# Gate products and sums moved to GpSimd, one product's bank emptied early, and the latent norm interleaved with the context's keys

## The chip, the cores and the metric

The kernel runs on one core of a Trainium2 chip. The metric is the device time of one execution in microseconds. A core has a matrix engine (PE, with its weight loads listed as PEld), a vector engine (DVE), a scalar engine (ACT), GpSimd (POOL) and DMA engines that are fed from queues; SP only issues DMAs, ACT and POOL issue DMAs beside their own work. Each engine takes its instructions in one fixed order and stands where an instruction has to wait.

## The reference

A trunk of two layers over 256 latent tokens and 256 context tokens of width 1024. Layer 0 is a bidirectional mLSTM with a gated ConvFFN, for context and latents; layer 1 is multi-head latent attention with a gated ConvFFN, for the latents alone. What the change touches is this:

```
x1 = layer_norm(ALPHA * x + gate * mixer(h))             # for both streams, layer 0
f  = (silu(dwconv(h2 @ W_gate)) * (h2 @ W_up)) @ W_out
x2 = layer_norm(ALPHA * x1 + gate * f)
# layer 1, latents: q, k, v from h3 = x2 * (1 + scale) + shift, context keys and values from hc
ckv, k_rope = split(h @ w_dkv);  k, v = split(rms_norm(ckv) @ w_ukv)
q = rms_norm(h3 @ w_dq) @ w_uq
```

Each layer norm ends in `* g + b`. The kernel folds that into the modulation for the next product and, apart from it, writes the full `x = z * g + b` to memory for the next residual.

## The kernel before, in words

Float32 products are made of three passes with split operands: every weight tile (128 x 1024) arrives by DMA as `raw`, ACT copies it to a rounded high part (L323) and DVE subtracts to get the low part (L326); `mm3` (L383 to L385) then multiplies high by high, high by low and low by high. So each weight tile costs an ACT pass, a DVE pass, and 12 matmuls of 512 columns on PE. A class `Stream` holds the order of the tiles, the ring of `raw` buffers and three split buffers `w` (NB = 3). A `raw` buffer comes free when DVE has split it; then SP issues the next load.

The tile framework has a scheduler: it orders each engine's instructions by its own estimate of costs, except where `keep_in_program_order` (here `pin`) holds an instruction in the place where the program wrote it. Background work (norms, transposes) is written as generators, and `tick` runs one step of them between products.

**`w_fout0`** (from L1365) is the output product of layer 0's ConvFFN, done as a Strassen-like scheme of seven products on 512-column halves. First come four products side by side, `yt2`, `y11`, `yt3` and `yt1`, six tiles each, into four pairs of PSUM banks p6, p1, p7 and p5 (all eight banks). Then the pairs are combined: ACT copies p1 to `u1` (L1434), DVE forms `u2`, `u3`, `v` and the final `u4` from PSUM (L1437 to L1446). Then follow `y21` (six tiles, 66 matmuls), `y22` (66) and `yt4` (three tiles, then three more kept for the end), each into a new pair of banks. A generator `residual` does, for each of eight half blocks, `u = u * gate` (L1454) and `z = ALPHA * z + u` (L1455) on DVE, one block per tick; for the blocks of `vv` it also takes the norm's statistics (`bn_stats`, L1457). `add` (L1464 to L1466) brings in `y21`, `y22` and at the very end `yt4`. `z_norm` (L1502 on) normalises, `ln_T` (L1191 on) transposes on PE and splits.

The weight tiles of `yt4` need a sum in memory: SP loads a stored partial sum (`t2d`, L278) and when that has landed POOL issues a DMA that adds the weights to it (L279). These issues stand in POOL's order.

**Layer 1's start.** `mla_ctx` makes the context's compressed keys, `ukn(0)` the context's keys of eight heads (48 matmuls of 256 columns), `uv` its values. Before, `ukn(0)` and `uv((0,))` are written first, and then four ticks of the latents' norm (`mid(1)`, that is `norm1`: add `yt4`, normalise, transpose, split into `hl`). Then `mla` multiplies `hl` by `w_dkv` (48 matmuls of 320 columns, `dkv`) and by `w_dq` (48 of 384, `dq`), transposes the latents' compressed keys (`dkv_T`, L1572 to L1577) and makes the latents' keys with `ukn(1)`.

**`ln_x`** (L1217) writes `z * g + b`: four products (L1227) and four sums (L1228) on DVE per call, each followed by a DMA from POOL. It is called with `ln` = 0 for both streams of layer 0's first norm, with 1 for the latents' second norm and with 2 in layer 1. **`ffn_in`** (L1292) in layer 1 uses for pair 0 of the columns three matmuls of 256 columns, and from pair 1 on two matmuls (L1320: one of 512 columns that serves high and low at once, one of 256), whose two halves ACT copies (L1323) and DVE adds (L1324).

Of the kernel before, what the change touches and what calls it, by code (L numbers as in the profile page):

```python
# [11 lines left out]
ALU = mybir.AluOpType  # L12
# [342 lines left out]
class K:  # L355
# [861 lines left out]
    def ln_x(self, ln, zs, dst):  # L1217


        nc = self.nc  # L1220
        g = self.bcast(self.a["ln_g"][ln:ln + 1, :], "gr")
        b = self.bcast(self.a["ln_b"][ln:ln + 1, :], "br")
        yield
        for t in range(2):
            for h in range(2):
                c = slice(h * 512, (h + 1) * 512)
                nc.vector.tensor_tensor(zs[t][:, c], zs[t][:, c], g[h], op=ALU.mult)  # L1227
                nc.vector.tensor_tensor(zs[t][:, c], zs[t][:, c], b[h], op=ALU.add)  # L1228
                nc.gpsimd.dma_start(dst[t][:, c], zs[t][:, c])
                yield  # L1230

# [60 lines left out]
    def ffn_in(self, l, hT, n, nt, pre=(), both=None):  # L1292

        nc, st = self.nc, self.st
        cw, cb = self.smc("fcw%d" % l), self.smc("fcb%d" % l)
        key = "fin%d" % l
        acts = []
        pre = list(pre)
        for p in range(NF):
            pss = []  # L1300
            for j in range(2):
                if pre:
                    w, ps = pre.pop(0)
                    self.ffn_half(ps, w, hT, 1)
                    if not pre:
                        st.unhold()
                else:
                    w = st.use((key, p, j))
                    ps = self.ps("fin")
                    two = ps.rearrange("p (a t) -> p a t", a=2)  # L1310
                    for k in range(8):
                        c = slice(k * 128, (k + 1) * 128)
                        hi, lo = hT(k)
                        if both is None or p == 0:
                            self.mm3(ps[:, :n], (w[0][:, c], w[1][:, c]), (hi, lo), k == 0, k == 7)
                            continue

                        mms = [(two, w[0][:, c], both(k)), (ps[:, :n], w[1][:, c], hi)]
                        for i, (o, a, b) in enumerate(mms if k < 7 else mms[::-1]):
                            nc.tensor.matmul(o, a, b, start=k == 0 and i == 0, stop=k == 7 and i == 1)  # L1320
                    if both is not None and p > 0:
                        t = self.s2("fs")
                        nc.scalar.copy(t[:, n:2 * n], ps[:, n:2 * n])  # L1323
                        nc.vector.tensor_tensor(t[:, :n], ps[:, :n], t[:, n:2 * n], op=ALU.add)  # L1324
                        ps = t
                pss.append(ps)
                self.tick(nt, ADA_F if p else 0)
            tmp = self.s2("fg")
            self.conv(pss[0], [cw[:, j * NF + p:j * NF + p + 1] for j in range(3)], cb[:, p:p + 1], tmp, n)
            nc.vector.tensor_tensor(tmp[:, :n], tmp[:, :n], pss[1][:, :n], op=ALU.mult)  # L1330
            if l == 0:
                if p % 2:
                    self.act_sums(p // 2, acts.pop(), tmp)
                else:
                    acts.append(tmp)
                continue
            a = self.u("act")
            nc.scalar.copy(a[:, 0, :n], tmp[:, :n])
            nc.vector.tensor_sub(a[:, 1, :n], tmp[:, :n], a[:, 0, :n])
            acts.append(a)  # L1340
        return acts
# [23 lines left out]
    def w_fout0(self, x1d, mid):  # L1365
# [25 lines left out]
        def prod(ps, x, w, i, bs=(0, 1)):  # L1391
            for h in range(2 if i < 5 else 1):
                j = 2 * i + h
                a = A[x, j]
                for b in bs:
                    ts = slice(b * 128, (b + 1) * 128)
                    cs = slice(h * 512, (h + 1) * 512)
                    self.mm3(ps[b], (a[:, 0, ts], a[:, 1, ts]), (w[0][:, cs], w[1][:, cs]), j == 0, j == 10)
# [4 lines left out]
        lo, hi = slice(0, 512), slice(512, 1024)  # L1403
        p6, p1, p7, p5 = [pair() for _ in range(4)]
        n = 0
        for i in range(6):
            for name, ps, x in (("yt2", p6, "S2"), ("y11", p1, "1"), ("yt3", p7, "S3"), ("yt1", p5, "S1")):
                w = st.use((name, 0, i))
                prod(ps, x, w, i)
                for f in ("S2", "1", "S3", "S1"):  # L1410
                    if f == x:
                        for j in (2 * i, 2 * i + 1):
                            A.pop((f, j), None)
                self.tick(1)
                if n >= 8:
                    operand()
                if n == 14:
                    gate = []
                    for g in (1, 0):
                        t = self.uf("gate")  # L1420
                        nc.gpsimd.dma_start(t, self.gd[0, 5][g:g + 1, :].to_broadcast([128, 1024]))
                        gate.append(t)
                if n >= 16 and n % 2 == 0:
                    if n == 16:
                        z = []
                    t = self.uf("z")
                    nc.gpsimd.dma_start(t, x1d[len(z)])
                    z.append(t)
                n += 1
        stats = [self.tiny(12, "st").rearrange("p (a b) -> p a b", b=6) for _ in range(4)]  # L1430
        u1, u3, u4, vv = [], [], [], []
        for b in range(2):
            u = self.s2("u1")
            nc.scalar.copy(u, p1[b])  # L1434
            u1.append(u)
            u = self.s2("u2")
            nc.vector.tensor_tensor(u, p6[b], u1[b], op=ALU.add)  # L1437
            u4.append(u)
# [7 lines left out]
            nc.vector.tensor_tensor(u4[b], p5[b], u4[b], op=ALU.subtract)  # L1446
            vv.append(v)

        def residual():

            for us, g, c in ((u1, 0, lo), (u4, 0, hi), (u3, 1, lo), (vv, 1, hi)):
                for b in range(2):
                    zz = z[2 * g + b]
                    nc.vector.tensor_tensor(us[b], us[b], gate[g][:, c], op=ALU.mult)  # L1454
                    nc.vector.scalar_tensor_tensor(zz[:, c], zz[:, c], ALPHA, us[b], op0=ALU.mult, op1=ALU.add)  # L1455
                    if us is vv:
                        nc.vector.bn_stats(stats[2 * g + b][:, 1], zz[:, c])  # L1457
                    yield

        def add(g, c, ps):  # L1460
            for b in range(2):
# [7 lines left out]
        for i in range(6):  # L1469
            w = st.use(("y21", 0, i))  # L1470
            prod(ps, "2", w, i)
            if i == 1:
                self.bg.append(residual())
            self.tick(1)
            operand()
        add(0, lo, ps)
        ps = pair()
        for i in range(6):
            w = st.use(("y22", 0, i))
            prod(ps, "S4", w, i)  # L1480
            self.tick(1)
            operand()
        self.drain()
# [4 lines left out]
        for i in range(6 - YTAIL):  # L1488
            w = st.use(("yt4", 0, i))
            prod(ps, "3", w, i)  # L1490
            self.tick(2)
        self.drain()
        mid(None, None, None)
        ws = [(i, st.use(("yt4", 0, i), hold=True)) for i in range(6 - YTAIL, 6)]
# [85 lines left out]
                nc.scalar.copy(self.krT[:, 0, cs], p)  # L1580
                nc.vector.tensor_sub(self.krT[0:64, 1, cs], p[0:64], self.krT[0:64, 0, cs])

    def ukn(self, g):

        cs = slice(g * 256, (g + 1) * 256)
        for h in range(H1):
            w = self.wk[h // 4]
            if h % 2 == 0:
                ps = self.ps("kn")
            hs = slice((h % 2) * 256, (h % 2 + 1) * 256)  # L1590
            for k in range(2):
                c = slice((h % 4) * 256 + k * 128, (h % 4) * 256 + (k + 1) * 128)
                self.mm3(ps[:, hs], (w[0][:, c], w[1][:, c]), (self.ckT[k][:, 0, cs], self.ckT[k][:, 1, cs]),
                         k == 0, k == 1)
            u = self.kn[h]
            self.split(u[:, 0, cs], u[:, 1, cs], ps[:, hs])

    def uv(self, ts):
        for t in ts:
# [33 lines left out]
    def mla(self, hl):  # L1633
# [7 lines left out]
        for c in range(4):  # L1641
            w = st.use(("dq", 0, c))
            self.tick()
            for kk in range(2):
                k = 2 * c + kk
                hi, lo = hl(k)
                cs = slice(kk * 384, (kk + 1) * 384)
                for t in range(2):
                    ts = slice(t * 128, (t + 1) * 128)
                    self.mm3(pss[t][:, :384], (hi[:, ts], lo[:, ts]), (w[0][:, cs], w[1][:, cs]), k == 0, k == 7)  # L1650
        cq = []
        for t in range(2):
            r = self.s2("cq")
            self.rms(pss[t][:, 0:384], 384, r[:, 0:384])
            cq.append(r)
        self.dkv_T(rows, 2)
        self.ukn(1)
        g = self.smc("qng")
        cqT = []
# [139 lines left out]
def build(tc, off, a, out):  # L1799
    es = ExitStack()  # L1800
    with es:
# [116 lines left out]
        k.tick(1)  # L1918
        st.pump(kv0 + PC)
        k.mla_kv()  # L1920
        k.ukn(0)
        k.uv((0,))
        k.tick(4)
        k.uv((1,))
        k.drain()
        k.take_late()
# [57 lines left out]
```

## Time and profile before

| what | value |
|---|---|
| median of three runs | 1386.9 us (1386.04 to 1388.71) |
| the profiled execution | 1386.22 us, span 1384.1 us, granted PE clock 0.996 |
| PE busy | 1354.0 us, 98% of the span |
| DVE busy | 1090.0 us, 79% |
| ACT busy | 713.1 us, 52% |
| POOL busy | 121.6 us, 9%, nearly all of it DMA issues |
| DMA | 297.58 MB, mean 215 GB/s |

In rows of the timeline the columns are the start in us, the duration in us, engine, line, operation, tiles written and read with shapes, a count, and in brackets the idle time before the instruction with what ended it. A row with a count merges neighbours. A matmul's duration is longer than its step: neighbours of 512 columns start 0.227 us apart. In the waits view a row gives who waited for whom, the total in us, the number of waits and the longest. In the view by windows each engine has its busy time in that stretch, and PEclk is the clock granted to PE.

### The profile page before, as it was taken

To read this page: it belongs to the slowest core of one execution; us is meant where nothing else is said; L and a number is where in the kernel's file an instruction comes from. 1 tells how busy PE (TensorE), PEld (TensorE's weight loads), DVE (VectorE), ACT (ScalarE), POOL (GpSimd) and SP (SyncE) were. 2 spreads that over 40 slices of the span, in tenths; PEclk is the share of its full clock that TensorE was granted. 3 is DMA by queue.
4 is the path that set the end of the run, shared out by engine and by line. 5 is a ranking of instruction groups with operands and counts; after the bars stand their busy time and mean duration, and the time that the engine had idled before them with its cause. 6 is when DMAs were issued, how large, how long until landed. Compare 5 with 4: busy or idle time off the path is not lost.

```text
span 1384.1 us, 18592 instructions
## 1 busy us (share of the span) xinstructions
PE 1354.0 (98%) x6567; PEld 1123.2 (81%) x6567; DVE 1090.0 (79%) x1768; ACT 713.1 (52%) x1221; POOL 121.6 (9%) x215
## 2 busy tenths in 40 slices
PE   7999999999999999999999999999999999999997
PEld 3788888888788888878898888888777888888886
DVE  6598857687688697779799878668898789788873
ACT  6585534435444555364643434334637567466660
POOL 0033000011011011120002000000001001000100
PEclk9999999999999999999999999999999999999999
DMA  9689847789666364766747877646987425256750
GB/s 338 227 293 316 290 156 247 239 286 302 214 200 204 105 232 132 250 193 228 241 147 239 300 230 234 212 145 229 312 231 226 137 99 202 109 185 185 252 202 31
DMA packets 97900, 297.58 MB, mean 215 GB/s; under 512 B 12136, under 2 KB 24808, under 8 KB 97808
## 3 DMA queue, kind: packets, MB, share of 16 engines
q1 hardware_dynamic: 68672, 218.52, 47.5%
q0 software_dynamic: 17472, 57.57, 13.3%
q10 hardware_dynamic: 11664, 20.32, 4.1%
q8 instruction: 51, 0.84, 0.2%
q14 instruction: 41, 0.34, 0.1%
HBM read 262.90 MB, written 33.46 MB: 214 GB/s over the span
## 4 chain that ended last, share of the span: by engine, by line
PE 91%; DVE 5%; ACT 2%; issue 1%; DMA 0%; SPq 0%; DVEq 0%; ACTq 0%
PE fin L1320 9%; PE fin L383 6%; PE fin L384 6%; PE fin L385 6%; PE tok L383 6%; PE tok L384 6%; PE tok L385 6%; PE y L384 5%; PE y L385 5%; PE y L383 5%; PE qk L383 4%; PE qk L385 4%; PE qk L384 4%; PE up L383 2%; PE up L385 2%; PE up L384 2%
## 5 line engine op out<-in xcount | busy, mean ns | idle before, releaser
L326 DVE TENSOR_TENSOR w<-raw,w 128x1024 fp32r<-128x1024 f32 (+3 forms) x290 | 348.1, 1203 | 141.3 <-ACT w L323 140.3
L323 ACT CAST w<-raw 128x1024 fp32r<-128x1024 f32 (+3 forms) x290 | 300.4, 1037 | 306.2 <-PE tok L385 88.6
L512 DVE SCALAR_TENSOR_TENSOR junk<-ar,bc 128x1024 f32<-128x1024 f32 x128 | 156.0, 1218 | 4.9 <-ACT bc L554 2.1
L384 PE MATMUL fin<-h,w 128*128 128x512 f32 (+1 forms) x376 | 141.2, 376 | 0.0
L385 PE MATMUL fin<-h,w 128*128 128x512 f32 (+1 forms) x376 | 140.9, 375 | 0.0
L383 PE MATMUL fin<-h,w 128*128 128x512 f32 (+1 forms) x376 | 140.8, 376 | 0.1
L1320 PE MATMUL fin<-h,w 128*128 128x256 f32 (+1 forms) x640 | 113.0, 339 | 0.0
L1320 PEld LDWEIGHTS fin<-h,w 128*128 128x128 f32 x640 | 98.2, 189 | 14.7
L383 PE MATMUL qk<-xc,w 128*128 128x512 f32 x256 | 100.7, 393 | 0.0
L385 PE MATMUL qk<-xc,w 128*128 128x512 f32 x256 | 99.9, 390 | 0.0
L384 PE MATMUL qk<-xc,w 128*128 128x512 f32 x256 | 99.8, 390 | 0.0
L384 PEld LDWEIGHTS fin<-h,w 128*128 128x128 f32 x376 | 70.8, 188 | 12.9 <-DVE h L1212 0.2
L385 PEld LDWEIGHTS fin<-h,w 128*128 128x128 f32 x376 | 70.8, 188 | 12.9
L383 PEld LDWEIGHTS fin<-h,w 128*128 128x128 f32 x376 | 70.5, 188 | 13.1 <-ACT h L1211 0.3
L383 PEld LDWEIGHTS qk<-xc,w 128*128 128x128 f32 x256 | 48.1, 188 | 10.0 <-issue 0.4
L385 PEld LDWEIGHTS qk<-xc,w 128*128 128x128 f32 x256 | 48.1, 188 | 9.9
L384 PEld LDWEIGHTS qk<-xc,w 128*128 128x128 f32 x256 | 48.1, 188 | 9.7
L383 PE MATMUL up<-hT,w 128*128 128x512 f32 x128 | 50.5, 394 | 0.5 <-ACT hT L388 0.5
L384 PE MATMUL up<-hT,w 128*128 128x512 f32 x128 | 50.1, 392 | 0.5 <-DVE hT L389 0.5
L385 PE MATMUL up<-hT,w 128*128 128x512 f32 x128 | 50.1, 391 | 0.3 <-DVE w L389 0.3
L383 PE MATMUL tok<-w,hT 128*128 128x512 f32 x128 | 49.8, 389 | 0.0
L384 PE MATMUL tok<-w,hT 128*128 128x512 f32 x128 | 49.8, 389 | 0.0
(463 smaller groups left out, 3151.2 us busy)
## 6 DMA issues: line engine op xcount, KB each, us to landing
raw<-in_ws SPq DMA_DIRECT2D x287, 512.0 KB, 4.3
ar<-in_adaT SPq DMA_DIRECT2D x80, 512.0 KB, 4.6
adaw<-in_ada_w SPq DMA_DIRECT2D x32, 256.0 KB, 6.7
t2d<-raw ACTq DMA_DIRECT2D x13, 512.0 KB, 4.9
raw<-t2d SPq DMA_DIRECT2D x13, 512.0 KB, 6.3
raw<-in_ws POOLq DMA_DIRECT2D x13, 512.0 KB, 8.0
zr<-fd ACTq DMA_DIRECT2D x33, 128.0 KB, 3.9
xmd<-xr POOLq DMA_DIRECT2D x16, 256.0 KB, 5.0
```

The lines of the kernel that those rows point to most:

```text
L323: k.nc.scalar.copy(h[:, :cols], src)
L326: k.nc.vector.tensor_sub(l[:, :cols], src, h[:, :cols])
L383: mm(out, w[0], x[0], start=start, stop=False)
L384: mm(out, w[0], x[1], start=False, stop=False)
L385: mm(out, w[1], x[0], start=False, stop=stop)
L512: nc.vector.scalar_tensor_tensor(o, w, 1.0, self.bc[j], op0=ALU.mult, op1=ALU.mult, accum_out=col[:, k, j:j + 1])
L1320: nc.tensor.matmul(o, a, b, start=k == 0 and i == 0, stop=k == 7 and i == 1)
```

## The change

Six edits, independent of each other in the code:

1. `ln_x`: for `ln` 1 and 2 the four products and four sums run on GpSimd. For `ln` 0 they stay on DVE, but each also multiplies by ALPHA, so that the stored x1 already carries the factor of the residual.
2. `w_fout0`: `u1` is copied from p1 right after the last tile of `y11`, pinned, and no longer after all four products.
3. `w_fout0`: `residual` is no generator any more. Its eight products and eight sums (the sums without ALPHA) run on GpSimd, pinned in four groups: `u1` and `u4` ahead of `y21`, `u3` after tile 4 of `y21`, `vv` after tile 1 of `y22`.
4. The two `bn_stats` of the `vv` blocks are written after the first three tiles of `yt4`, unpinned.
5. `ukn(0)` ticks the latents' norm after heads 1, 3 and 5, with one tick left after `uv((0,))`; in `mla`, `dkv_T` of the latents moves from behind `dq` to ahead of `dq`'s last contraction step.
6. `ffn_in` in layer 1: column pair 1 also uses the three matmuls of 256 columns, without the copy and sum behind them.

```
             for h in range(2):
                 c = slice(h * 512, (h + 1) * 512)
-                nc.vector.tensor_tensor(zs[t][:, c], zs[t][:, c], g[h], op=ALU.mult)
-                nc.vector.tensor_tensor(zs[t][:, c], zs[t][:, c], b[h], op=ALU.add)
+                zz = zs[t][:, c]
+                if ln:
+                    nc.gpsimd.tensor_tensor(zz, zz, g[h], op=ALU.mult)
+                    nc.gpsimd.tensor_tensor(zz, zz, b[h], op=ALU.add)
+                else:
+                    nc.vector.scalar_tensor_tensor(zz, zz, ALPHA, g[h], op0=ALU.mult, op1=ALU.mult)
+                    nc.vector.scalar_tensor_tensor(zz, b[h], ALPHA, zz, op0=ALU.mult, op1=ALU.add)
                 nc.gpsimd.dma_start(dst[t][:, c], zs[t][:, c])
...
-                        if both is None or p == 0:
+                        if both is None or p < 2:
...
-                    if both is not None and p > 0:
+                    if both is not None and p > 1:
...
+                if (name, i) == ("y11", 5):
+                    for b in range(2):
+                        u = self.s2("u1")
+                        pin(nc.scalar.copy(u, p1[b]))
+                        u1.append(u)
...
-            u = self.s2("u1")
-            nc.scalar.copy(u, p1[b])
-            u1.append(u)
...
-        def residual():
-
-            for us, g, c in ((u1, 0, lo), (u4, 0, hi), (u3, 1, lo), (vv, 1, hi)):
-                for b in range(2):
-                    zz = z[2 * g + b]
-                    nc.vector.tensor_tensor(us[b], us[b], gate[g][:, c], op=ALU.mult)
-                    nc.vector.scalar_tensor_tensor(zz[:, c], zz[:, c], ALPHA, us[b], op0=ALU.mult, op1=ALU.add)
-                    if us is vv:
-                        nc.vector.bn_stats(stats[2 * g + b][:, 1], zz[:, c])
-                    yield
+        def residual(us, g, c):
+
+            for b in range(2):
+                zz = z[2 * g + b][:, c]
+                pin(nc.gpsimd.tensor_tensor(us[b], us[b], gate[g][:, c], op=ALU.mult))
+                pin(nc.gpsimd.tensor_tensor(zz, zz, us[b], op=ALU.add))
+        residual(u1, 0, lo)
+        residual(u4, 0, hi)
...
             w = st.use(("y21", 0, i))
             prod(ps, "2", w, i)
-            if i == 1:
-                self.bg.append(residual())
+            if i == 4:
+                residual(u3, 1, lo)
...
             w = st.use(("y22", 0, i))
             prod(ps, "S4", w, i)
+            if i == 1:
+                residual(vv, 1, hi)
...
             w = st.use(("yt4", 0, i))
             prod(ps, "3", w, i)
             self.tick(2)
+        for b in range(2):
+            nc.vector.bn_stats(stats[2 + b][:, 1], z[2 + b][:, hi])
...
-    def ukn(self, g):
+    def ukn(self, g, steps=()):
...
             self.split(u[:, 0, cs], u[:, 1, cs], ps[:, hs])
+            if h in steps:
+                self.tick(1)
...
                     self.mm3(pss[t][:, :384], (hi[:, ts], lo[:, ts]), (w[0][:, cs], w[1][:, cs]), k == 0, k == 7)
+                if k == 6:
+                    self.dkv_T(rows, 2)
...
-        self.dkv_T(rows, 2)
         self.ukn(1)
...
-        k.ukn(0)
+        k.ukn(0, (1, 3, 5))
         k.uv((0,))
-        k.tick(4)
+        k.tick(1)
```

The scheduler places the unpinned instructions anew. In the changed kernel's built order, DVE, POOL and PE have these stretches (`u3`, `vv`, `z` and `w` as in the code; the numbers in `w` and `raw` tell tiles apart):

```
DVE   L326 w (y22, tile 4)                       POOL  L1460, L1461 x4 each: u1, u4 (8 passes)
      L1500 bn_stats of z, vv block 0, waits POOL      L279 raw (yt4 tile 0), L279 raw (yt4 tile 1)
      L1500 bn_stats of z, vv block 1, waits POOL      L1460, L1461, L1460: u3 (3 passes)
      L326 w (y22, tile 5)                             L279 raw (yt4 tile 2)
      L326 w (yt4, tile 0)                             L1461: u3; L1460, L1461, L1460, L1461: vv (5 passes)
PE    yt4's last matmul, 6 x kn, 1 x zT (needs z of block 0 normalised), 12 x kn,
      7 x zT (needs block 1), 6 x kn, 4 x zT, 24 x kn and 24 x v with the last 4 x zT among them, dkv
```

Before, the same place on PE reads: yt4's last matmul, then 24 x kn and 8 x v, 2 x zT, 3 x v, 6 x kn, 1 x v, 10 x zT, 6 x kn, 4 x zT, and the rest of kn and v ahead of dkv.

More of the change, by code (lines that the diff above doesn't have):

```diff
@@ L1405, in w_fout0 @@
         n = 0
+        u1, u3, u4, vv = [], [], [], []
         for i in range(6):
@@ L1429, in w_fout0 @@
                 n += 1
+                if (name, i) == ("y11", 5):
[3 more added lines that the diff above has]
+                        u1.append(u)
         stats = [self.tiny(12, "st").rearrange("p (a b) -> p a b", b=6) for _ in range(4)]
-        u1, u3, u4, vv = [], [], [], []
         for b in range(2):
-            u = self.s2("u1")
-            nc.scalar.copy(u, p1[b])
-            u1.append(u)
             u = self.s2("u2")
```

## The prediction

> **What bounds the kernel now.** I read the page first, then the waits of PE, then the busy times by window where these waits lie, and last the timelines of those stretches, engine by engine. The page's first lines:
>
> ```profile
> span 1384.1 us, 18592 instructions
> PE 1354.0 (98%) x6567; PEld 1123.2 (81%) x6567; DVE 1090.0 (79%) x1768; ACT 713.1 (52%) x1221; POOL 121.6 (9%) x215
> ```
>
> PE is busy 98%, and no edit takes real work from it. All that can be won are PE's waits. Those that the edits reach, from PE's waits view:
>
> ```profile
> PE y L384 <- DVE w L326: 3.2, 3, 1.4
> ...
> PE y L383 <- ACT u L1434: 1.5, 1, 1.5
> PE dkv L383 <- ACT hl L1211: 1.5, 1, 1.5
> ...
> PE kn L383 <- ACT ckT L1576: 0.7, 1, 0.7
> ```
>
> Of the first row's 3.2 us, 1.1 lie in another stage (the other two waits are shown below with 0.76 and 1.35). So 5.8 us of waits can go, 0.4% of the time: no large gain is open. The windows show who sets the pace there:
>
> ```profile
> 1002.00:1015.00 13.00, 12.11 (x51) 9.40 (x52) 12.96 (x20) 6.35 (x10) 0.00 (x0) 1.00 0.64 219
> 1015.00:1030.00 15.00, 13.65 (x61) 10.94 (x60) 15.00 (x22) 5.49 (x6) 2.65 (x3) 1.00 0.89 234
> 1080.00:1095.00 15.00, 15.00 (x87) 15.00 (x87) 13.35 (x30) 7.79 (x16) 2.18 (x4) 0.90 0.60 211
> ```
>
> The third busy time is DVE's: in `y21` and `y22` it has no free time, so DVE's order decides when weights are split. The last row shows a granted clock of 0.90 behind the latent norm's wait.
>
> **Edit 2, bank of `y11` emptied early.** Where `y21` begins:
>
> ```profile
> 997.69 1.05 ACT L323 CAST w<-raw 128x1024 fp32r<-128x1024 f32 x1
> ...
> 1001.27 0.58 ACT L1434 COPY u<-y 128x512 f32<-128x512 f32 x1
> ```
>
> ```profile
> 998.78 1.23 DVE L326 TENSOR_TENSOR w<-raw,w 128x1024 fp32r<-128x1024 f32 x1 [0.53 <-ACT w L323]
> 999.92 0.69 DVE L1387 TENSOR_TENSOR fz<-zr,fz 128x512 fp32r<-128x512 f32 x1
> ...
> 1002.98 0.69 DVE L1454 TENSOR_TENSOR u<-u,gate 128x512 f32<-128x512 f32 x1
> 1003.59 0.68 DVE L1437 TENSOR_TENSOR u<-y,u 128x512 f32<-128x512 f32 x1
> ...
> 1007.77 2.35 DVE L326 TENSOR_TENSOR w<-raw,w 128x1024 fp32r<-128x1024 f32 x2
> ```
>
> ```profile
> 1001.90 0.50 PE L383 MATMUL y<-w,fz 128*128 128x512 f32 x1 [1.53 <-ACT u L1434]
> ...
> 1009.04 0.50 PE L384 MATMUL y<-w,fz 128*128 128x512 f32 x1 [0.76 <-DVE w L326]
> ...
> 1025.88 0.50 PE L384 MATMUL y<-w,fz 128*128 128x512 f32 x1 [1.35 <-DVE w L326]
> ```
>
> With p1's banks free, PE could begin `y21` at 1000.2. But the two copies now stand on ACT ahead of the cast that began at 997.69 and push it by about 1.0, and DVE's first split of `y21` with it, to an end at 1001.0. Then DVE has, at steps of 0.60 a 512-column pass and 1.14 a split: operand, sum, split, operand, sum, six more sums, split: 10 x 0.60 + 2 x 1.14 = 8.3, so `y21`'s third tile is split at 1009.3. Before, it was at 1008.9 (half of the last row's pair), and PE stood for it until 1009.04. The early start is spent waiting for the third tile: edit 2 moves the wait, +0.3 at this point. Then 41 matmuls x 0.227 = 9.3 bring `y21` to its end at 1018.7, before 1018.4.
>
> **Edits 3 and 4, the residual on GpSimd.** DVE loses eight products and eight sums at 0.60, 9.6 us of queue, and `y22` can run without the wait of 1025.88: PE would reach its last tile at 1018.7 + 60 x 0.227 = 1032.3. But the two `bn_stats` of `vv` now stand on DVE between the splits of tile 4 and tile 5 of `y22`, and wait for GpSimd. GpSimd's price and queue:
>
> ```profile
> L1164 POOL TENSOR_TENSOR z<-z,gr 128x512 f32<-128x512 f32 x1 | 1.4, 1425 | 61.1 <-ACT z L1163 61.1
> ```
>
> ```profile
> 1018.62 0.89 POOL L279 DMA_DIRECT2D raw<-in_ws  x1 [44.38 <-DVE w L326]
> 1022.84 0.89 POOL L279 DMA_DIRECT2D raw<-in_ws  x1 [3.33 <-DVE z L1455]
> 1028.62 0.87 POOL L279 DMA_DIRECT2D raw<-in_ws  x1 [4.89 <-DVE w L326]
> ```
>
> ```profile
> L278 SPq DMA_DIRECT2D raw<-t2d x1: 326/326/326, 1019.9 to 1019.9; - x1
> ...
> DMA to landing us min/median/max: 8.1/8.1/8.1
> ```
>
> The third L279 row is the one that counts: its partial sum was issued by SP at 1019.9, when DVE had split tile 1 of `y22`, and landed 8.1 later; POOL's issue followed at 1028.62. In the changed order one pass of `u3` and four of `vv` stand behind this issue. Tile 1 is split behind `add`'s first product, which needs `y21`'s end: 1018.7 + 0.60 + 1.14 = 1020.4; landing 8.1 later and 0.6 to POOL as before: 1029.1. Then 0.87 for the issue and five passes of 1.42 with gaps of 0.07 (as the two GpSimd rows under the rivals start): 8.3, so `vv` is done at 1037.4. Then `bn_stats` 0.60 and the half-width split 0.60: tile 5 is there at 1038.7, and PE, which was ready at 1032.5, stands 6.2 us. `y22` ends five matmuls later, at 1039.9; before, it ended 41 matmuls after 1025.88, at 1035.2. That is +4.7.
>
> Bounds. If the partial sum landed at once after SP's issue, the queue would still hold: the second L279 cannot be before about 1021.6 (its load goes out behind tile 0's split, 1016.8 now, and took 4.7 from 1018.18 to 1022.84), and 2 x 0.87 plus eight passes at 1.49 make 13.7, so 1035.3 and +2.6 in all. With landings as late as the longest of this stretch,
>
> ```profile
> DMA to landing us min/median/max: 5.4/8.0/10.9
> ```
>
> it is 2.8 more, +7.5. I take +4.7, since the row in question is that load itself. What is queued behind the waiting DVE are the splits of `yt4`'s tiles 0 and 1 and `add`; they come 1.14 apart and PE needs them 1.4 and 2.7 later, so nothing is added, and the context's norm, which is bound by DVE and follows the same splits, simply comes 4.7 later. The first eight passes (`u1`, `u4`) end near 1013, ahead of the first L279, and delay no issue.
>
> **Edit 5, latent norm between the keys.** From the end of `yt4` to `dkv`:
>
> ```profile
> 1061.47 0.28 PE L383 MATMUL kn<-ckT,wu 128*128 128x256 f32 x1
> 1061.58 0.28 PE L384 MATMUL kn<-ckT,wu 128*128 128x256 f32 x1
> ...
> 1078.41 0.42 PE L383 MATMUL dkv<-w,hl 128*128 128x320 f32 x1 [1.51 <-ACT hl L1211]
> ...
> 1087.45 0.51 PE L383 MATMUL dq<-w,hl 128*128 128x384 f32 x2
> ```
>
> ```profile
> 1066.36 0.54 DVE L1513 TENSOR_SCALAR z<-z,mv,rs 128x512 f32<-128x512 f32 x1
> ...
> 1068.49 0.54 DVE L1513 TENSOR_SCALAR z<-z,mv,rs 128x512 f32<-128x512 f32 x1
> ```
>
> The two normalised blocks are ready 5.5 and 7.6 after `yt4`'s end, and DVE's order up to there is unchanged. The new PE order has only six key matmuls (0.7) ahead of the first transpose, so PE stands 4.7 us, then does twelve (1.4), stands until 7.6, and has 10.8 of work left: `dkv` starts 18.4 after `yt4`'s end instead of 16.9. In return `hl` is ready by then. The old `dkv` took 9.0 from 1078.41 to 1087.45, with its first third at half pace; the context's took 7.1, so 1.9 comes back. A stand of 4.7 will cost clock in its turn, as the shorter one did before; I put 0.8 for that. Together +0.4, between -1.9 (the norm is ready by the first transpose after all) and +3.
>
> `dkv_T` ahead of `dq`'s last step:
>
> ```profile
> 1095.80 0.82 PE L1572 MATMUL ckT<-ident,ckr 128*128 128x128 f32 x6
> 1097.37 0.74 PE L383 MATMUL kn<-ckT,wu 128*128 128x256 f32 x4 [0.75 <-ACT ckT L1576]
> ```
>
> Six matmuls of `dq` (1.0) now cover ACT's evacuation: -0.9, or 0 if the rows of DVE come just late.
>
> **Edits 1 and 6.**
>
> ```profile
> 1136.46 0.55 POOL L1269 DMA_DIRECT2D xres<-x2d  x1 [48.89 <-PE qrT L1720]
> ```
>
> ```profile
> L1320 PEld LDWEIGHTS fin<-h,w x640: 187/188/192, 1202.1 to 1314.7; 128*128 128x128 f32 x160
> ```
>
> `ln_x` with `ln` 1 and 2 takes eight passes of 0.60, 4.8 us per call, from DVE, after the transposes, where PE has work of its own. On POOL a call is 8 x 1.42 = 11.4 us, and the next load behind it there stood idle for 48.89 us before: that covers it for `ln` 1, and for `ln` 2 the result is read only after the whole of `ffn_in`. For `ln` 0 a pass with the factor costs DVE what one without did. In `ffn_in`, three 256-column matmuls at 0.12 (the key matmuls' step) replace a pair at 112.6/320 = 0.352, 16 times: +0.1. All: +0.1; the cover is PE's own work.
>
> **Sum**: +4.7 + 0.4 - 0.9 + 0.1 = +4.3 on the profiled execution's 1386.2: 1390.5. The median of the runs stands 0.7 above that execution.
>
> **The rivals.** *DVE and GpSimd hold each other up.* Eleven of the passes run while DVE has splits to do. Ahead of `y21`'s third tile, five DVE passes read two SBUF tiles, and each may stand behind a pass of 1.42: up to 7.1, half of it on the average, so 1394. The one place to look:
>
> ```profile
> 1375.13 0.42 DVE L1142 SCALAR_TENSOR_TENSOR z<-xres,z 128x256 f32<-128x256 f32 x1
> ...
> 1376.79 0.43 DVE L1142 SCALAR_TENSOR_TENSOR z<-xres,z 128x256 f32<-128x256 f32 x1
> ```
>
> ```profile
> 1373.78 1.43 POOL L1164 TENSOR_TENSOR z<-z,gr 128x512 f32<-128x512 f32 x1 [61.11 <-ACT z L1163]
> 1375.28 1.42 POOL L1165 TENSOR_TENSOR z<-z,br 128x512 f32<-128x512 f32 x1
> ```
>
> The first DVE pass lies across GpSimd's two, the second behind them, and they take 0.42 and 0.43. So the sum has 0 for it, but the overlap is 0.4 us long and decides little. The Trainium skill, "SBUF — State Buffer", section "Who interferes with whom", states that a DVE instruction with two SBUF inputs contends with a GpSimd instruction that reads SBUF, and that the later one blocks fully. By that rule this rival is right; the trace's one overlap does not show it.
>
> *Faster: `vv` is done before PE needs tile 5.* If GpSimd is through by 1031, for instance because its passes overlap their start-up or the scheduler's order bites less than I read, `y22` runs free: the wait of 1025.88 goes (1.7), with `dkv_T` 0.9 and the latent norm's 1.9: 1382. The deciding point is `vv` done ahead of tile 5. The queue above speaks against it.
>
> *No change.* The partial sum lands at its earliest (+2.6) and the latent norm and `dkv_T` give 2.8: 1386.
>
> **How the numbers follow.** Main case 0.53, contention 0.19, faster 0.14, no change 0.14. A difference of 0.2%, 2.8 us, is about what a measurement can tell here. Of the main case some 0.06 lie within it: slower 0.66, same 0.20, faster 0.14. The range for eight in ten goes from 1384.5, inside the no-change case, to 1397, the contention case with most of its 7.1; the main case alone has 1388 to 1393.5.
>
> **What would show it.** Right: a PE wait of 4 to 8 us at `y` L384 on a DVE split near 1033 to 1039, with DVE's `bn_stats` (L1500) waiting for POOL just ahead; a PE wait of over 4 us at `zT`; no wait of `dkv` on `hl`, none of `kn` on `ckT`. Contention would show as DVE splits well over 1.23 or GpSimd passes well over 1.43. Wrong: `bn_stats` without a wait, or `y22`'s last tile without one.

## The result, and the profile after

The changed kernel takes 1406.5 us in the median of four runs (1405.64 to 1407.99), the kernel before 1386.47 in the same comparison: the ratio is 1.0144, with a 95% interval of 1.0126 to 1.0162. It is slower by 20 us where +4.3 was forecast, and lies beyond the range. The profiled execution took 1405.84 with a span of 1404.1.

The page's first lines, and below them PE's waits in the changed kernel (total in us, number of waits, longest):

```profile
span 1404.1 us, 18631 instructions
...
PE 1361.0 (97%) x6583; PEld 1129.7 (80%) x6583; DVE 1087.1 (77%) x1734; ACT 713.2 (51%) x1219; POOL 169.0 (12%) x247
```

```profile
PE y L384 <- DVE w L326: 10.6, 3, 5.2
...
PE zT L1199 <- issue: 4.6, 1, 4.6
PE fin L384 <- DVE h L1212: 3.5, 4, 1.4
PE kn L383 <- DVE kn L389: 2.4, 2, 2.0
```

Thirty-two passes left DVE, and its busy time hardly fell, from 1090.0 to 1087.1: what stayed on it took longer. The first row of waits grew from 3.2 to 10.6 us. The wait at `zT` was foreseen, the last two rows were not. (`issue` means that the view names nothing that ended the wait; DVE's pass that normalises the block, L1522, ends at 1078.06, and the transpose starts at 1078.16.)

The timelines of DVE and of POOL where the first two products run beside GpSimd's residual, and at the start of layer 1's `ffn_in`:

```profile
1009.85 1.95 DVE L326 TENSOR_TENSOR w<-raw,w 128x1024 fp32r<-128x1024 f32 x1
1011.72 1.75 DVE L1392 TENSOR_TENSOR fz<-zr,fz 128x512 fp32r<-128x512 f32 x1
...
1029.01 3.96 DVE L326 TENSOR_TENSOR w<-raw,w 128x1024 fp32r<-128x1024 f32 x2
1038.91 0.69 DVE L1500 BATCH_NORM_STATS2 st<-z 128x6 f32<-128x512 f32 x1 [5.95 <-POOL z L1461]
...
1204.39 4.67 DVE L1212 TENSOR_TENSOR h<-zm,h 128x256 fp32r<-128x256 f32 x4
```

```profile
1029.73 2.15 POOL L1461 TENSOR_TENSOR z<-z,u 128x512 f32<-128x512 f32 x1
1031.85 2.28 POOL L1460 TENSOR_TENSOR u<-u,gate 128x512 f32<-128x512 f32 x1
1034.07 0.88 POOL L279 DMA_DIRECT2D raw<-in_ws  x1
```

The same group of four `h` splits in the kernel before:

```profile
1189.79 1.42 DVE L1212 TENSOR_TENSOR h<-zm,h 128x256 fp32r<-128x256 f32 x4
```

A weight split takes 1.95 where it took 1.23, a pair 3.96 where it took 2.35, an operand's split 1.75 where it took 0.69, the four `h` splits 4.67 where they took 1.42. GpSimd's passes go from 1.42 to 2.15 and 2.28. Each engine waits for the other's pass. PE's rows show what follows:

```profile
1011.85 0.79 PE L384 MATMUL y<-w,fz 128*128 128x512 f32 x1 [4.37 <-DVE w L326]
```

```profile
1002.00:1015.00 13.00, 8.63 (x31) 6.65 (x31) 13.00 (x14) 5.25 (x7) 11.65 (x8) 0.83 0.61 207
1044.00:1057.00 13.00, 12.87 (x56) 10.09 (x54) 10.12 (x19) 7.29 (x10) 4.34 (x6) 0.84 0.95 242
```

The stand at `y21`'s third tile was 0.76 before. The granted clock is 0.83 in the window that holds this stand, and 0.84 in the one that begins just behind the stand of 5.2 us in `y22`. By stage, from the first matmul of each in the two traces: the key matmuls after `yt4` begin 11.2 later than before (1072.65 against 1061.47), the first scores 13.9 later (1132.35 against 1118.44), the first `ffn_in` matmul of layer 1 14.6 later, and 20 us are reached when its second part begins.

### The profile page after: what moved, and what is told of

Same layout as the page of the kernel before. It is cut to its first block, busy times and chain, and to the rows that moved or that the text cites. A ratio compares the mean times of both kernels' runs of the same rounds, so it can differ in the third digit from the quotient of the medians.

```text
span 1404.1 us, 18631 instructions
## 1 busy us (share of the span) xinstructions
PE 1361.0 (97%) x6583; PEld 1129.7 (80%) x6583; DVE 1087.1 (77%) x1734; ACT 713.2 (51%) x1219; POOL 169.0 (12%) x247
## 4 chain that ended last, share of the span: by engine, by line
PE 86%; DVE 6%; DMA 4%; ACT 2%; issue 1%; POOL 1%; SPq 0%; ACTq 0%; DVEq 0%; POOLq 0%
PE fin L1325 8%; PE fin L384 6%; PE fin L383 6%; PE fin L385 6%; PE tok L383 6%; PE tok L385 6%; PE tok L384 6%; PE y L384 4%; PE y L385 4%; PE qk L383 4%; PE qk L385 4%; PE qk L384 4%; PE y L383 4%; PE up L383 2%; PE up L384 2%; PE up L385 2%
## 5 line engine op out<-in xcount | busy, mean ns | idle before, releaser
L1325 PEld LDWEIGHTS fin<-h,w 128*128 128x128 f32 x640 | 98.1, 189 | 14.6
```

## The experiments

All are compared with the kernel before on the same chip, whose median was 1386.0 (first four runs), 1385.8 (next four) and 1386.3 (last four).

| label | what is in it | median us | less before | ratio, 95% |
|---|---|---|---|---|
| e1_lnx_alone | edit 1 for `ln` 1 and 2 | 1392.65 | +6.7 | 1.0032 to 1.0063 |
| e2_lnx_memset | the same, GpSimd only writes | 1384.88 | -1.1 | 0.9984 to 1.0003 |
| e3_resid_alone | edits 3 and 4 | 1394.29 | +8.3 | 1.0036 to 1.0069 |
| e4_resid_bnlate | the same, `bn_stats` late | 1388.63 | +2.6 | 1.0013 to 1.0032 |
| e5_no_gpsimd | edits 2, 5, 6 | 1390.54 | +4.7 | 1.0018 to 1.0042 |
| e6_latent_alone | edit 5 | 1389.16 | +3.3 | 1.0010 to 1.0029 |
| e7_u1_alone | edit 2 | 1387.69 | +1.9 | 1.0006 to 1.0024 |
| e8_u1_dkvT | edit 2, and `dkv_T` of edit 5 | 1385.49 | -0.3 | 0.9990 to 1.0008 |
| e9_lnx_oneread | as e1, GpSimd reads one tile | 1385.40 | -0.9 | 0.9982 to 1.0000 |
| e10_lnx_memset3 | as e2, three times as many | 1385.69 | -0.6 | 0.9990 to 1.0008 |
| e11_dkvT_alone | `dkv_T` of edit 5 | 1385.13 | -1.2 | 0.9980 to 0.9998 |
| e12_ticks_later | edit 5, ticks after heads 5, 7 | 1390.12 | +3.8 | 1.0017 to 1.0035 |

Theory: DVE's and GpSimd's passes that read two SBUF tiles block each other, and this, with the stand behind GpSimd's queue, makes the loss. Rivals: the queue alone, as the prediction had it; or the orders of edits 2 and 5.

### Edit 1 alone, and GpSimd that only writes

```
-                nc.vector.tensor_tensor(zs[t][:, c], zs[t][:, c], g[h], op=ALU.mult)
-                nc.vector.tensor_tensor(zs[t][:, c], zs[t][:, c], b[h], op=ALU.add)
+                if ln:
+                    nc.gpsimd.tensor_tensor(zz, zz, g[h], op=ALU.mult)     # e2: nc.gpsimd.memset(zz, 0.0)
+                    nc.gpsimd.tensor_tensor(zz, zz, b[h], op=ALU.add)      # e2: nc.gpsimd.memset(zz, 0.0)
...
```

> The kernel before with edit 1 alone: the products and sums of ln_x for ln 1 and 2 on GpSimd, those of ln 0 untouched. Theory (DVE's passes with two SBUF inputs and GpSimd's passes block each other): the four splits of the h tiles at the start of the second ffn_in, 1.42 and 1.43 us per group of four before, take over 4 us again as in the changed kernel, PE waits there some 3.5 us in all, runs at a lower granted clock behind it, and with a smaller part in mla the time is 1393 (1391 to 1395). Rival (the prediction's term: PE's own work covers it): 1386.6, within 1 us of the kernel before.

> As the run before, but each of GpSimd's passes in ln_x for ln 1 and 2 is a memset of the same tile: it writes 128 x 512 and reads nothing (so x2 and x3 are left out of the computation, stored as zeros). Theory in its narrow form (the blocking comes from GpSimd's reads): the groups of h splits stay at 1.4 us and the time is within 1.5 us of the kernel before, 1386.5. Rival a (any work of GpSimd that touches SBUF blocks DVE): groups of over 2.5 us and 1389 to 1393. Rival b (it is the queue of loads behind GpSimd's passes, not the passes): as in the run before, as far as memset takes as long.

The first took 1392.65, +6.7, the second 1384.88. DVE and POOL of e1 at the start of `ffn_in`:

```profile
1191.62 4.66 DVE L1212 TENSOR_TENSOR h<-zm,h 128x256 fp32r<-128x256 f32 x4
...
1197.11 4.78 DVE L1212 TENSOR_TENSOR h<-zm,h 128x256 fp32r<-128x256 f32 x4
```

```profile
1190.43 4.15 POOL L1229 TENSOR_TENSOR z<-z,gr 128x512 f32<-128x512 f32 x3 [24.12 <-PE zT L1199]
1194.55 2.87 POOL L1230 TENSOR_TENSOR z<-z,br 128x512 f32<-128x512 f32 x2
```

Here GpSimd runs at its own pace (4.15 for three) and DVE gets about one short split in for each of its passes. The two groups take 9.4 us instead of 2.85. PE needs these splits at once. From the first `fin` matmul to the first whose weights the profile names `w` and not `wu`, it needs 18.2 us (1191.47 to 1209.70) where it needed 12.7 (1189.64 to 1202.30): 5.6 of the 6.7 us. Only 2.7 of that are waits; between them the matmuls run slower, as the granted clock (0.91 and 0.81) in the windows of the kernel before and of e1 shows at the same place:

```profile
1185.00:1203.00 18.00, 15.83 (x101) 14.13 (x100) 13.58 (x33) 9.27 (x22) 2.18 (x4) 0.91 0.13 48
```

```profile
1185.00:1203.00 18.00, 12.68 (x69) 10.45 (x68) 14.51 (x24) 7.71 (x17) 12.45 (x11) 0.81 0.16 63
```

By these two clocks some 1.8 us of the 18 are lost to the slower pace (an estimate: 0.19 less 0.09 of 18); the remaining 1.1 is not split up further.

A memset takes only 0.5 us, so e2 could have missed the splits for being short. Two more runs take that away.

### Passes that read one tile, and longer writing

```
-                    nc.gpsimd.tensor_tensor(zz, zz, g[h], op=ALU.mult)
-                    nc.gpsimd.tensor_tensor(zz, zz, b[h], op=ALU.add)
+                    nc.gpsimd.tensor_scalar(zz, zz, 1.0, None, op0=ALU.mult)   # e9, twice
+                    for _ in range(6): nc.gpsimd.memset(zz, 0.0)               # e10
```

> As the run with edit 1 alone, but each of GpSimd's passes in ln_x for ln 1 and 2 reads one tile and not two: a multiplication of z by 1.0 in its place (so the factor g and the summand b of these two norms are left out of x2 and x3). Theory (any GpSimd pass that reads SBUF blocks DVE's two-input passes for as long as it lasts): the groups of four h splits at the second ffn_in stay over 2.5 us, and the time is 1389 to 1394, less than with edit 1 only as far as a pass is shorter than 1.35 us. Rival (it takes two inputs on GpSimd's side too): groups of 1.4 us, 1386 (1385 to 1387).

> As the run with memsets, with three memsets in the place of one: GpSimd is busy with writing for 24 x 0.5 = 12 us per call, as long as with the sixteen reading passes of edit 1 (x2 and x3 are left out again, stored as zeros). Theory (reads block, writes don't): groups of h splits at 1.4 us, 1385.5 (1384.5 to 1387). Rival (the single memsets were only too short to be met): groups of over 2 us and 1388 or more.

They took 1385.40 and 1385.69, no loss in either. (Edit 1 has eight passes per call, some 11 us, and not the sixteen of the expectation; e10's writing lasts as long all the same.) DVE and POOL of e10:

```profile
1189.10 1.42 DVE L1212 TENSOR_TENSOR h<-zm,h 128x256 fp32r<-128x256 f32 x4
...
1191.35 1.42 DVE L1212 TENSOR_TENSOR h<-zm,h 128x256 fp32r<-128x256 f32 x4
```

```profile
1187.89 2.85 POOL L1230 MEMSET z<- 128x512 f32 x6 [41.88 <-PE zT L1199]
```

and of e9:

```profile
1188.87 1.85 DVE L1212 TENSOR_TENSOR h<-zm,h 128x256 fp32r<-128x256 f32 x4
...
1191.55 1.42 DVE L1212 TENSOR_TENSOR h<-zm,h 128x256 fp32r<-128x256 f32 x4
```

```profile
1187.71 2.94 POOL L1229 TENSOR_SCALAR z<-z 128x512 f32<-128x512 f32 x2 [41.96 <-PE zT L1199]
1190.62 1.48 POOL L1230 TENSOR_SCALAR z<-z 128x512 f32<-128x512 f32 x1
1192.08 2.24 POOL L1229 TENSOR_SCALAR z<-z 128x512 f32<-128x512 f32 x1
```

In e10 the first group lies wholly within GpSimd's memsets and keeps its 1.42 us. In e9 GpSimd's pass is longer than in e1 (1.48 against 1.38), it reads SBUF, and yet the groups take 1.85 and 1.42, not 4.7; only one split of the eight was late by 0.4, and one GpSimd pass by 0.8. So it isn't GpSimd's being busy, nor its writing. My theory was too wide for e9: the strong form of the blocking was seen only where GpSimd, too, reads two tiles. Why a pass with one input met DVE so much less isn't settled by these runs.

### Edits 3 and 4 alone, with and without the stand behind GpSimd

```
+        def residual(us, g, c):     # as in the change, on GpSimd; u1 copied where it was before
...
         for b in range(2):
-            nc.vector.bn_stats(stats[2 + b][:, 1], z[2 + b][:, hi])          # e3, as in the change
+            pin(nc.vector.bn_stats(stats[2 + b][:, 1], z[2 + b][:, hi]))     # e4
```

> The kernel before with edits 3 and 4 alone: residual on GpSimd, bn_stats of vv written later (and ALPHA folded into ln_x for ln 0, at the same number of DVE passes). Theory (mutual blocking and the queue together): splits of 1.9 to 2.3 us in y21 and y22, PE standing 3 to 4.5 us for the third tile of y21 and about 5 us for the last of y22, and half pace behind both: 10 us in that stage, 1396.5 (1394 to 1399). Rival (the queue alone, as the prediction had it): one stand of 6 us in y22, 1391.2.

> As the run before, but the two bn_stats of vv are pinned, so that DVE meets them only after the splits of the context's norm, and no weight split stands behind GpSimd's queue. Theory (mutual blocking): the stand in y22 goes, the late third tile of y21 with its half pace stays, and splits beside GpSimd passes still take about 2 us: 1390.5 (1388.5 to 1393). Rival (the queue alone): nothing is left of the loss and the wait of the kernel before at 1025.88 goes too: 1385 (1384 to 1386.5).

They took 1394.29 (+8.3) and 1388.63 (+2.6). PE's wait row and DVE's rows in e3:

```profile
PE y L384 <- DVE w L326: 9.9, 4, 6.2
```

```profile
1008.30 0.68 DVE L1453 TENSOR_TENSOR v<-y,u 128x512 f32<-128x512 f32 x1
1008.90 0.68 DVE L1454 TENSOR_TENSOR u<-y,u 128x512 f32<-128x512 f32 x1
1009.50 2.15 DVE L326 TENSOR_TENSOR w<-raw,w 128x1024 fp32r<-128x1024 f32 x1
...
1037.88 0.69 DVE L1501 BATCH_NORM_STATS2 st<-z 128x6 f32<-128x512 f32 x1 [5.89 <-POOL z L1462]
```

and in e4, the same wait row and the late splits of `y22`, and what GpSimd did beside them:

```profile
PE y L384 <- DVE w L326: 5.1, 4, 2.4
```

```profile
1026.61 6.39 DVE L326 TENSOR_TENSOR w<-raw,w 128x1024 fp32r<-128x1024 f32 x3
1033.30 3.62 DVE L326 TENSOR_TENSOR w<-raw,w 128x1024 fp32r<-128x1024 f32 x1 [0.31 <-ACT w L323]
```

```profile
1033.02 1.56 POOL L1462 TENSOR_TENSOR z<-z,u 128x512 f32<-128x512 f32 x1
1034.27 1.56 POOL L1461 TENSOR_TENSOR v<-v,gate 128x512 f32<-128x512 f32 x1
1035.90 2.16 POOL L1462 TENSOR_TENSOR z<-z,v 128x512 f32<-128x512 f32 x1
```

The stand of 6.2 us in `y22` goes with the place of `bn_stats`, and 5.7 us of the 8.3 with it. What is left, 2.6, is put down to the blocking, since no weight split stands behind GpSimd's queue any more and yet a single split of 3.62 us, three times its length, lies across two of GpSimd's passes and reaches into the third. The queue alone would have left nothing, so that rival falls; the size came out a little under the 4.5 expected. PE's longest wait in e4 is not where the expectation had it, at `y21`'s third tile, but later in `y21`, behind an operand's splits of 3.49 us for two and a weight split of 2.29 (e3 has it too, 2.44 us):

```profile
1017.11 0.50 PE L384 MATMUL y<-w,fz 128*128 128x512 f32 x1 [2.37 <-DVE w L326]
```

The half pace that was expected behind it is missing in both: the granted clock from 1017 to 1027 is 1.00.

In e3, GpSimd's order shows what `bn_stats` waited for:

```profile
1026.46 0.89 POOL L279 DMA_DIRECT2D raw<-in_ws  x1 [3.50 <-DVE w L326]
...
1033.08 0.88 POOL L279 DMA_DIRECT2D raw<-in_ws  x1
```

From the second L279 on, GpSimd works without a pause until 1040.40: two issues and eight passes, some of them stretched to 2.27. The third L279 did not wait for its partial sum to land. The first two of e3's DVE rows show the other side: a pass that takes one operand from PSUM (`y`) keeps its 0.68, with GpSimd at work beside it (its passes there took 1.30).

### The parts without GpSimd

```
# e5: edits 2, 5 and 6;  e6: edit 5;  e7: edit 2;  e8: edit 2 and
+                if k == 6:
+                    self.dkv_T(rows, 2)
         cq = []
...
-        self.dkv_T(rows, 2)
         self.ukn(1)
```

> The kernel before with edits 2, 5 and 6: all of the change but the passes on GpSimd (edits 1, 3 and 4). Edits 1 and 3 with 4 alone cost 6.7 and 8.3 us, the whole change 20.5, so 5.5 us are left. Theory (they arise only where edits 2 and 5 meet GpSimd's passes: a longer stand with a lower clock behind it at y21's third tile, and ln_x reaching the splits of hl and kn earlier): 1386.5 (1385 to 1388). Rival (edits 2, 5 and 6 cost that by themselves): 1391.5 (1390 to 1393).

> The kernel before with edit 5 alone. The prediction's term: PE stands 4.7 us at the first zT, dkv begins 18.4 us after the end of yt4 against 16.9, the stages behind give it back, 1385.5 in all. Theory after the trace of the changed kernel: dkv begins some 20.4 after (22.3 there, of which 2.0 is a wait for a kn split that stood behind GpSimd), 3.5 us lost, dkv without half pace and the covered dkv_T give back 3: 1386.5 (1385.5 to 1387.5). Rival (the 2.7 us that the changed kernel lost between yt4's end and the first scores are the order's own): 1389.

> The kernel before with edit 2 alone. The prediction's term: the wait for the banks of p1 goes, and the gain is spent waiting for y21's third tile, 1386.3 to 1386.8, no change. Rival (the wait is won, as its row in the waits of PE reads): 1384.5.

> The kernel before with edit 2 and, of edit 5, only dkv_T ahead of dq's last step: the two parts with no GpSimd pass and no earlier norm. Theory: the wait of kn on ckT goes, -0.9, and edit 2 gives nothing: 1385.3 (1384.3 to 1386.3). Rival (dkv_T stands for DVE's rows): 1386.5 or more.

They took 1390.54, 1389.16, 1387.69 and 1385.49. In e5 and e6 the theory lost to its rival: edits 2, 5 and 6 cost 4.7 us by themselves, edit 5 by itself 3.3. In e7 neither was right: edit 2 by itself costs 1.9. e8 lies within its expectation, but its difference of -0.3 is no change that can be told. The losses add: 6.7 (e1) + 8.3 (e3) + 4.7 (e5) = 19.7, the change 20.0. So the total needs no meeting of the parts, as far as the intervals allow (e1's alone is 4.3 us wide). One is in the trace of the change all the same, and in no other: PE waits 2.0 us for a key split that stands on DVE behind two splits of `hl`, and these take 2.90 beside `ln_x`'s passes on GpSimd, where two take 0.75 in e6.

```profile
1092.83 0.39 PE L383 MATMUL kn<-ckT,wu 128*128 128x256 f32 x1 [2.00 <-DVE kn L389]
```

```profile
1089.54 2.90 DVE L1212 TENSOR_TENSOR hl<-zm,hl 128x256 fp32r<-128x256 f32 x2
```

In e7 PE stands 2.52 us for the third tile of `y21` where it had stood 0.76, and runs behind it at 0.83:

```profile
1011.51 0.62 PE L384 MATMUL y<-w,fz 128*128 128x512 f32 x1 [2.52 <-DVE w L326]
```

```profile
1010.00:1020.00 10.00, 8.48 (x30) 6.88 (x31) 10.00 (x15) 3.27 (x6) 0.00 (x0) 0.83 0.59 167
```

In e6, from the waits of PE, and DVE's timeline ahead of `dq`:

```profile
PE zT L1199 <- issue: 4.6, 1, 4.6
PE dq L384 <- DVE w L326: 1.1, 1, 1.1
```

```profile
1086.25 1.28 DVE L1227 TENSOR_TENSOR z<-z,gr 128x512 f32<-128x512 f32 x2
...
1089.86 1.28 DVE L1228 TENSOR_TENSOR z<-z,br 128x512 f32<-128x512 f32 x2
1091.06 0.95 DVE L326 TENSOR_TENSOR w<-raw,w 128x768 fp32r<-128x768 f32 x1
```

`dkv` begins 19.8 us after the first key matmul (1063.62 to 1083.45), before 16.9; `dkv` itself is 2.0 shorter; and then PE waits 1.1 for a weight of `dq`, since the norm's end came earlier and so `ln_x`'s eight passes now lie on DVE ahead of `dq`'s split. From the first key matmul to the first scores e6 needs 58.5, the kernel before 57.0. That is 1.5 of the 3.3. But the trace of the kernel before is one of those in which `dkv` runs slowly. PE stands 1.5 us ahead of it in all ten traces that leave the norm where it was. In five of them (before, e1, e4, e7, e11) the granted clock over the next 4 us was 0.63 to 0.79, and `dkv` took 9.0 to 9.5 us; in the other five (e2, e3, e8, e9, e10) the clock was 1.00 and `dkv` took 7.4 to 7.5. The window around `dkv` in e11 and in e8, where this part of the program is the same:

```profile
1080.00:1090.00 10.00, 9.90 (x55) 9.64 (x55) 8.99 (x18) 5.92 (x14) 2.17 (x4) 0.83 0.35 110
```

```profile
1080.00:1090.00 10.00, 9.45 (x60) 9.11 (x61) 10.00 (x21) 6.65 (x17) 2.18 (x4) 1.00 0.27 94
```

So the 2.0 us are only in part the edit's. From the first key matmul to the first scores e2, e3, e9 and e10, with `dkv` at full clock, need 55.3 to 55.5, and against them edit 5 loses 3.0 to 3.2. Why the clock fell in one trace and not in the other isn't shown.

### What of edit 5 is worth keeping

> The kernel before with, of edit 5, only dkv_T ahead of dq's last step. The prediction's term is -0.9 (or 0): the wait of 0.7 of kn on ckT goes. In the run with edit 2 beside it the stretch from the first key matmul to the first scores took 54.7 us against 57.0, 1.5 of it in dkv, which ran there without half pace. Theory: 1384.9 (1384 to 1385.5). Rival (the half pace of dkv is chance and the wait moves to the next product): 1385.8, no change.

The edit is the one shown for `dkv_T` above, by itself.

```
-        k.ukn(0)
+        k.ukn(0, (5, 7))       # e12, with dkv_T moved too
         k.uv((0,))
-        k.tick(4)
+        k.tick(2)
```

> As edit 5 alone, but ukn(0) ticks the norm after heads 5 and 7 and no sooner, with two ticks left after uv((0,)): 18 key matmuls instead of 6 stand ahead of the first zT. Theory (edit 5's loss is PE's stand at the first zT, which comes before the norm is ready, and the half pace behind it): the stand shrinks from 4.6 to 3.2 us, 12 matmuls fewer lie behind it at half pace or wait for banks, 1387 (1385.5 to 1388.3) against 1389.2. Rival (the norm's transposes among the keys cost it, wherever they begin): 1389.

e11 took 1385.13, ratio 0.9989 (0.9980 to 0.9998): a gain of 1.2 us whose interval ends just below no change. It is the only version with the whole computation of which as much can be said (e2, e9 and e10 leave out the products and sums of two norms). Its trace has no wait of `kn` on `ckT`. e12 took 1390.12, no better than edit 5. The stand at `zT` did shrink, and `dkv` began 18.1 after the first key matmul instead of 19.8, but the scheduler then put the `ckT` transposes earlier into `dq`, and PE stood for DVE's rows:

```profile
PE zT L1199 <- DVE z L1513: 2.7, 2, 2.2
...
PE ckT L1572 <- DVE ckr L1524: 2.0, 1, 2.0
```

So the expectation for e12 was right in its first half and failed on the next wait.

## Why the prediction was wrong

The sign was right and the size was not. The parts measured alone add up to 19.7 us, 15.4 more than forecast. Of these, 9.3 are the blocking, which the sum had at 0 (6.7 in e1, 2.6 in e4), 3.8 are edit 5 with `dkv_T`, 2.9 are the stands that edits 2 to 4 make (7.6 in place of 4.7), and edit 6 by subtraction takes 0.6 off. Step by step:

- *Edits 1 and 6, +0.1: wrong.* Edit 1 alone costs 6.7 us, the second largest term. The step that failed is "the cover is PE's own work". At the second `ffn_in` PE's work is the matmuls that need the `h` splits at once, and these stand on DVE behind GpSimd. Edit 6 was not run alone; e5 less e6 and e7 leaves -0.5 for it, which is nothing that can be told.
- *Edits 3 and 4, +4.7: the stand right, its path and the size wrong.* The stand in `y22`, forecast with 6.2 us, was 6.2 in e3 and 5.2 in the whole change, with L1500 waiting 5.95 for POOL just ahead. It is worth 5.7 us (e3 less e4). The blocking, costed at 0, adds 2.6. That the 6.2 came out is in part luck: the sum has the third L279 wait for its partial sum and five passes of 1.42 behind it, so that `vv` is done 37.2 us after `y21`'s start; in e3 it is done 37.2 after it as well (1003.24 to 1040.40), but there the third L279 stood behind three passes of 1.64 to 2.27 and not for the landing, and the five passes behind it were faster.
- *The two engines hold each other up, costed at 0, as a rival 0.19 and 1394: this is the step that decided.* I took 0 from the one overlap in the trace, 0.4 us long, though the text itself said that it decides little. The rival's place was right (splits of 1.95 to 2.3 and passes of 2.15 to 2.28 beside `y21` and `y22`), but it looked at the eleven passes there only; the larger part came from `ln_x`, which it left out. The Trainium skill, "SBUF — State Buffer", section "Who interferes with whom", names the condition: a DVE instruction with two SBUF inputs against a GpSimd instruction that reads SBUF, not one that only writes. e1 against e10 (4.7 against 1.42) agrees. In e9 GpSimd reads one tile and the groups stay at 1.85 and 1.42; there the measurement is narrower than the rule.
- *Edit 2, +0.3: place right, size wrong.* Forecast: the third tile at 1009.3 if `y21` starts at 1000.2. In e7 `y21` starts at 1002.25 and the tile is there at 1011.5, the same 9.1 to 9.3 later. But the stand of 2.5 us was taken to cost only itself against the wait it replaced; the clock of 0.83 behind it, some 1.7 us of 10 (an estimate from the window), was not counted. It cost 1.9 in e7. The 0.3 is part of the 4.7 above.
- *Edit 5 with `dkv_T`, +0.4 - 0.9: half right.* The stand of 4.7 at the first `zT` is there with 4.6, and `dkv_T` by itself gives 1.2 (0.9). `dkv` is 2.0 shorter than in the trace before (1.9 forecast), but with its stage unchanged it was 1.5 shorter in five of ten traces too: the forecast took one trace's slow `dkv` for the rule. But `dkv` starts 2.9 later, not 1.5: in e6 the twelve key matmuls behind the stand took 2.9 us (1069.24 to 1072.14) where I had 1.4 and a pause, and what followed took 11.3 in place of 10.8. And `dq`'s weights came late by 1.1, since I had not followed what an earlier norm does to `ln_x` on DVE. Together +3.3 (e6, `dkv_T` included) in place of -0.5.
- *Clock.* I charged 0.8 for a lower clock once, in edit 5. Behind every stand of over 4 us that the edits made, the clock over the next 4 us was 0.50 to 0.60 (4.4 and 5.2 in the change, 6.2 in e3, 4.6 at `zT`); the matmuls start 0.43 apart there, where they start 0.23 apart otherwise. Behind shorter stands it fell in some traces only: after 2.5 us to 0.83 over 10 us in e7, but after 2.5 in e5 and after 2.4 in e3 and e4 it stayed at 1.00. In e1 it was 0.81 where several waits of under 0.8 came together, with matmuls of half the width 0.21 apart in place of 0.12.

The forecast for the rivals "faster" and "no change" rested on GpSimd being done in time, and fell with it.

## What to carry to other kernels

Moving elementwise work from DVE to GpSimd isn't free where both read two SBUF tiles at the same time: ask which DVE passes will run beside it, and whether PE waits for those at once; passes that read PSUM on DVE, or GpSimd work that only writes, ran side by side here. Price a new stand of PE with the clock that may follow: here it fell to half or little more behind every new stand of over 4 us, and behind those of 1.5 to 2.5 us in some traces and not in others; e7's stand of 2.5 us, which replaced smaller waits, cost 1.9 net. A stretch that runs at a lower clock in one trace may not do so in the next, so a gain that rests on it wants more than one trace. When a sum has a zero that rests on an overlap too short to tell, carry the rival's price instead, through every place where the moved work runs.

## What was not expected of the hardware

- DVE gets about one short pass in for each of GpSimd's: four splits of 0.42 took 4.66 beside three passes that kept their 1.38. Beside longer DVE passes both stretch: splits of 1.22 took 1.95 to 3.62, GpSimd's passes up to 2.28.
- A GpSimd pass with one SBUF input (1.48 us) hardly touched the same splits, one with two inputs (1.38) tripled them.
- In e1 four waits of 0.4 to 0.8 us, 2.7 in all, beside the 1.8 at `zT` that the kernel before has as well, went with a clock of 0.81 in the window, against 0.91.
- The same stand of 1.5 us ahead of `dkv` was followed by a clock of 0.63 to 0.79 over 4 us in five traces and of 1.00 in five.
